# A token mixer whose normalised input is made once, split anew, and read by nearly all of its products

## The chip, the cores and the metric

The kernel runs on one core of one Trainium2 chip. The time is the device time of one execution in microseconds (us); of several runs the median counts. The five engines of the core are TensorE (PE in the profile), VectorE (DVE), ScalarE (ACT), GpSimd (POOL) and SyncE (SP), which issues most of the DMAs. Each engine works through its own instructions in the order in which they are written and waits at the first one whose inputs or buffers are not ready.

## The reference, cut to what matters

A decoder trunk of two layers over 512 tokens and 1024 features, in fp32. In each layer the mixer normalises its input, multiplies it by one wide matrix, and cuts the columns of the result into the inputs of three branches and three gates:

```python
def rmsnorm(x, w):
    r = lax.rsqrt(jnp.mean(xf * xf, axis=-1, keepdims=True) + EPS)
    return (xf * r * w.astype(jnp.float32)).astype(x.dtype)

def hybrid_mix(u, w_in, ...):
    (u_s5, q, k, v, g_out, gate_lr, z, xbc, dt_raw,
     gate_s5, gate_gla, gate_ssd) = jnp.split(u @ w_in, split_pts, axis=-1)
    y_s5 = s5_mixer(u_s5, ...)
    y_gla = gla_mixer(q, k, v, g_out, gate_lr, ...)
    y_ssd = ssd_mixer(z, xbc, dt_raw, ...)
    merged = (jax.nn.sigmoid(gate_s5) * (y_s5 @ w_br_s5)
              + jax.nn.sigmoid(gate_gla) * (y_gla @ w_br_gla)
              + jax.nn.sigmoid(gate_ssd) * (y_ssd @ w_br_ssd))
    return merged @ w_out

for i in range(DEPTH):
    h = h + 0.5 * swiglu(rmsnorm(h, ffn1_norm[i]), ...)
    h = h + hybrid_mix(rmsnorm(h, mix_norm[i]), w_in[i], ...)
    h = h + 0.5 * swiglu(rmsnorm(h, ffn2_norm[i]), ...)
    h = h + sigmoid(rmsnorm(h, ple_norm[i]) @ ple_gate[i]) * (p[i] @ ple_proj[i])
```

S5 is a diagonal state-space model with a gated output, GLA a gated linear attention in chunks, SSD the Mamba-2 mixer with a short convolution.

## The kernel before

Features lie on the 128 partitions and the 512 tokens along the row, so one tile of a feature block is 128x512. The residual h is eight such tiles. Each fp32 product is made of three matmuls of a faster type: both operands are split into a high and a low part, and `mm3` (L214, L219, L220) adds high by high, high by low and low by high. A pair of output tiles with 1024 inputs is 48 such matmuls of 512 columns.

Weights stream from memory over SyncE's queue into `raw` (three buffers); ScalarE makes the high part `wh` (L187) and VectorE the low part `wl` (L188). Products go into five PSUM banks `ps`; smaller work shares three banks `pa`. Tiles in SBUF come from a fixed set of slots (`self.T`, `self.free`), so a tile can also wait for the last reader of the slot that it gets.

The norm's root r is not applied to the input of the mixer's products. `prenorm` splits the input times the norm's weight at once, without r, into X (high parts `xh`, low parts `xl`), so that the products can begin before r is known. r, spread over all partitions, is multiplied in where a result leaves PSUM: by VectorE in `plain` (L1104, with a factor L1106), in `uev` (L1122, which also transposes) and in `gate` (L1230); the gate's Tanh is then ScalarE's (L1231).

`spread` brings a row of roots to all partitions: ScalarE and VectorE make `hl`, VectorE a diagonal `dg` (L288), TensorE multiplies it by ones (L290), and ScalarE copies the result (L292). Ahead of it `colsum` sums squares by TensorE (L271) and VectorE transposes the sums (L273). GLA's output o goes through both, is multiplied by the spread root `rb` (L1181), and split into `yh` and `yl` for its branch product.

S5 goes through eight blocks. In a block TensorE makes the states' inputs (L722), ScalarE and VectorE turn and scan them (`xsw`, `W`, `Hh`), and TensorE reads them a block later (L703) into Y, which ScalarE copies (L708). After blocks 3 and 7 eight DMAs write Y to memory (L711). Four loads (L756) bring it back as `y5`; gelu is two ScalarE and two VectorE steps a tile (L764 to L767), the result is split into `ggh` and `ggl`, and these feed the gated product (`s5_glu`). In SSD, `w` is made by ScalarE (L1055, L1056) and VectorE (L1057) and read by L1067.

The mixer's order of emission is a table written by hand, `ORDER`. A name in it is a unit (`lrdt`, `v0`, `kq0`, `bc0`, `x0`, `z0`, `glu` and so on), or one further step of a generator: `g0`, `g1` for GLA's halves, `st` for the SSD states, `s5_`, `s0`, `s1` for the SSD groups, `A`, `B`, `C` for the branches of GLA, S5 and SSD. A scheduler then places the instructions of all engines; it may move ready products between others. The units marked `first` are placed ahead of others that are ready.

Of the kernel before, what the change touches and what calls it, by code (L numbers as in the profile page):

```python
# [94 lines left out]
class Trunk:  # L95
# [988 lines left out]
    def mix(self, l, prep):  # L1084
# [135 lines left out]

        def branch(bi, Y):

            c0, wn = ((D, "w_br_gla"), (0, "w_br_s5"), (2 * D, "w_br_ssd"))[bi]
# [187 lines left out]
```

## Time and profile before

| | us |
|---|---|
| median of three runs | 2515.77 (2513.34 to 2517.47) |
| profiled execution | 2515.53 |
| its span | 2513.4 |
| TensorE busy | 2480.5 |
| VectorE busy | 1685.9 |
| ScalarE busy | 1041.3 |
| GpSimd busy | 50.1 |

Busy times are those of one execution and overlap; an engine at 99% of the span leaves 33 us in which it stood still. Matmuls are pipelined, so a matmul's own duration in a row is longer than the step from one to the next.

### The profile page before, as it was taken

The page shows a single profiled execution, that of the slowest core. Times are in us where ns is not written, and L with a number is a line of the kernel's source. Part 1 is how long each engine was busy: PE and PEld are TensorE (multiplying, and loading weights), DVE is VectorE, ACT ScalarE, POOL GpSimd, SP SyncE. Part 2 cuts the span into 40 slices and gives each one's busy share as a digit, 9 for nine tenths or more (in the row PEclk, how much of TensorE's full clock was granted, in tenths as well). Part 3 has the DMA queues.
Part 4 walks back from the last instruction along what each step waited for, and adds up shares of the span by engine and source line. Part 5 has one row for each costly group of instructions (what it writes and reads, how often), then busy time and mean ns, then how long its engine had stood idle before and what let it go on. Part 6 is the DMA issues. An engine that isn't in the chain of part 4 may idle for free.

```text
span 2513.4 us, 34868 instructions
## 1 busy us (share of the span) xinstructions
PE 2480.5 (99%) x12724; PEld 2044.5 (81%) x12724; DVE 1685.9 (67%) x4087; ACT 1041.3 (41%) x1889; POOL 50.1 (2%) x101
## 2 busy tenths in 40 slices
PE   9999999989999999999999999999899999999998
PEld 7888888868888888888888888888688888888888
DVE  7866778987776544445787577789876755434556
ACT  5323345545544433234533233455465434322354
POOL 0000000010000000000000000000100000000000
PEclk9999999989999999999999999999999999999999
DMA  4444345344223333333334444553442222323242
GB/s 166 126 132 125 114 132 150 115 140 144 90 84 101 100 93 101 93 92 97 109 101 121 131 129 118 155 126 110 145 142 91 86 101 93 101 93 101 79 127 76
DMA packets 164525, 284.54 MB, mean 113 GB/s; under 512 B 88321, under 2 KB 94337, under 8 KB 164353
## 3 DMA queue, kind: packets, MB, share of 16 engines
q1 hardware_dynamic: 157824, 261.31, 34.6%
q0 software_dynamic: 6528, 21.01, 2.6%
q8 instruction: 99, 1.62, 0.3%
q14 instruction: 74, 0.60, 0.1%
HBM read 258.64 MB, written 23.63 MB: 112 GB/s over the span
## 4 chain that ended last, share of the span: by engine, by line
PE 96%; DVE 2%; DMA 0%; issue 0%; ACT 0%; SPq 0%; DVEq 0%; ACTq 0%
PE ps L214 30%; PE ps L219 30%; PE ps L220 30%; PE ps L1168 1%; PE ps L1167 1%; PE ps L1166 1%; PE pa L849 1%; PE pa L703 1%; PE pa L1067 0%; PE pa L271 0%; DMA raw<-in_w 0%; PE pa L909 0%; DVE attn L855 0%; PE pa L722 0%; PE ps L217 0%
## 5 line engine op out<-in xcount | busy, mean ns | idle before, releaser
L188 DVE TENSOR_TENSOR wl<-raw,wh 128x512 fp32r<-128x512 f32 (+1 forms) x856 | 579.3, 678 | 574.0 <-ACT wh L187 567.9
L187 ACT ACTIVATE wh<-raw 128x512 fp32r<-128x512 f32 (+1 forms) x856 | 531.1, 622 | 996.3 <-PE ps L220 919.3
L214 PE MATMUL ps<-xh,wh 128*128 128x512 f32 (+1 forms) x2336 | 898.7, 385 | 0.9 <-ACT wh L187 0.9
L219 PE MATMUL ps<-xh,wl 128*128 128x512 f32 (+1 forms) x2336 | 898.2, 385 | 0.0
L220 PE MATMUL ps<-xl,wh 128*128 128x512 f32 (+1 forms) x2336 | 896.8, 384 | 0.0
L214 PEld LDWEIGHTS ps<-xh,wh 128*128 128x128 f32 x2336 | 439.0, 188 | 89.6 <-issue 1.5
L219 PEld LDWEIGHTS ps<-xh,wl 128*128 128x128 f32 x2336 | 439.1, 188 | 87.5 <-issue 1.5
L220 PEld LDWEIGHTS ps<-xl,wh 128*128 128x128 f32 x2336 | 438.9, 188 | 87.1 <-DVE xl L303 0.5
L214 PE MATMUL ps<-hdh,wh 128*128 128x512 f32 x704 | 274.3, 390 | 0.0
L220 PE MATMUL ps<-hdl,wh 128*128 128x512 f32 x672 | 261.5, 389 | 0.0
L219 PE MATMUL ps<-hdh,wl 128*128 128x512 f32 x672 | 261.4, 389 | 0.0
L214 PEld LDWEIGHTS ps<-hdh,wh 128*128 128x128 f32 x704 | 132.1, 188 | 28.4 <-issue 1.2
L220 PEld LDWEIGHTS ps<-hdl,wh 128*128 128x128 f32 x672 | 126.1, 188 | 26.3
L219 PEld LDWEIGHTS ps<-hdh,wl 128*128 128x128 f32 x672 | 126.1, 188 | 26.1
L343 ACT ACTIVATE s<-g 128x512 f32<-128x512 f32 x88 | 55.5, 631 | 100.3 <-DVE g L342 100.2
L227 ACT ACTIVATE hdh<-hd 128x512 fp32r<-128x512 f32 x88 | 55.5, 630 | 91.7 <-DVE hd L345 91.7
L344 DVE TENSOR_TENSOR u<-ps,r 128x512 f32<-128x512 f32 x88 | 60.6, 689 | 36.7 <-PE ps L220 36.2
L231 DVE TENSOR_TENSOR hdl<-hd,hdh 128x512 fp32r<-128x512 f32 x88 | 60.6, 688 | 31.8 <-ACT hdh L227 31.5
L214 PE MATMUL ps<-yh,wh 128*128 128x512 f32 x192 | 75.8, 396 | 0.1
L219 PE MATMUL ps<-yh,wl 128*128 128x512 f32 x192 | 75.1, 391 | 0.0
L220 PE MATMUL ps<-yl,wh 128*128 128x512 f32 x192 | 74.1, 394 | 0.0
L342 DVE TENSOR_TENSOR g<-ps,r 128x512 f32<-128x512 f32 x88 | 60.5, 688 | 7.8 <-ACT r L292 6.1
(381 smaller groups left out, 2544.9 us busy)
## 6 DMA issues: line engine op xcount, KB each, us to landing
raw<-in_w SPq DMA_DIRECT2D x414, 512.0 KB, 3.5
mat<-st SPq DMA_DIRECT2D x64, 64.0 KB, 2.3
mat<-toep SPq DMA_DIRECT2D x16, 256.0 KB, 2.2
mat<-cs SPq DMA_DIRECT2D x16, 256.0 KB, 3.4
raw<-in_w SPq DMA_DIRECT2D x16, 256.0 KB, 2.6
St<-mat POOLq DMA_DIRECT2D x16, 256.0 KB, 4.1
CS<-mat POOLq DMA_DIRECT2D x16, 256.0 KB, 4.6
Tt<-mat POOLq DMA_DIRECT2D x16, 256.0 KB, 4.8
```

The source lines that it names most:

```text
L187: nc.scalar.activation(H, x, AF.Copy)
L188: nc.vector.tensor_tensor(L, x, H.bitcast(F32), ALU.subtract)
L214: mm(ps, H[:, j, c], XH[k], start=(k == 0), stop=False)
L219: mm(ps, L[:, j, c], XH[k], start=False, stop=False)
L220: mm(ps, H[:, j, c], XL[k], start=False, stop=(k == nk - 1))
L227: nc.scalar.activation(H, x, AF.Copy)
L231: nc.vector.tensor_tensor(L, x, H.bitcast(F32), ALU.subtract)
L342: nc.vector.tensor_tensor(g1, pg, r[:p], ALU.mult)
L343: nc.scalar.activation(s, g1, AF.Silu)
L344: nc.vector.tensor_tensor(u1, pu, r[128 - p:], ALU.mult)
L703: nc.tensor.matmul(py[j:j + 64, g * 64:g * 64 + 64], x[:, g * 128 + j:g * 128 + j + 64], y, start=x is Tt, stop=x is Ot)
L849: nc.tensor.matmul(ps[o:o + 64, c * 64:c * 64 + 64], d[:, c * 128 + o:c * 128 + o + 64], P.rearrange("p (f c b j) -> p c b f j", f=2, c=4, ...
```

## The change

A new unit `xn` makes the normalised input itself once r is there: for each of the eight feature blocks GpSimd multiplies h by r (`xt`), ScalarE rounds `xt` times the norm's weight to the high part, and VectorE takes the low part. All products through `feats` after it read this XN in place of X. `lrdt`, both `v` and `kq0` keep X, which a second new unit, `xo`, frees after `v1`. Results of products on XN need no r: `plain` and `uev` are then one ScalarE activation each, and a gate is one Tanh straight from PSUM. The gates are no longer made inside the branches but by three generators `gA`, `gB`, `gC`, and are kept until their branch takes them. The table is written anew.

```diff
--- before.py
+++ after.py
@@ -37,10 +37,12 @@
 HALVES = ((0, 12), (12, NF))
 
 
 ORDER = """
-    lrdt v0 kq0 g0 g0 st s5_ g0 g0 kq1 g0 s5_ g0 st g0 g1 off go0 g0 v1 g0 g0 g1 st g0 bc0 gla0 g1 g1 go1 g1 g1 g1
...
+    lrdt v0 kq0 xn g0 g0 st v1 xo s5_ g0 g0 kq1 g0 s5_ g0 st g0 g1 off go0 g0 g0 g0 g1 st g0 gA gla0 g1 g1 go1 g1 g1 gA
...
+    s0 s0 s5_ gB s0 s0 s5_ s0 s0 s5_ z1 glu cb1 s1 gB s1 s1 gB s1 s1 B s1 s1 B gC s1 s1 B gC s1 s1 B s1 gC gC C C C C
 """
 
 
@@ -1093,14 +1095,32 @@
         def feats(evac, *cols):
             W = self.wunit(*[("w_in", c) for c in cols])
             ps = [self.PS(), self.PS()]
-            self.mm3([(ps[j], c128(j)) for j in range(2)], W, X)
+            self.mm3([(ps[j], c128(j)) for j in range(2)], W, XN or X)
             with self.first():
                 for j in range(2):
                     evac(j, ps[j])
 
+        XN = []
+
+        def normal():
+
+            H, L = [], []
+            for k in range(KD):
+                t = self.T("xt")
+                nc.gpsimd.tensor_tensor(t, self.hs[k], r, ALU.mult)
+                H.append(self.T("xh", F32R))
+                L.append(self.T("xl", F32R))
+                w = vec[:, VEC["mix"]][:, k:k + 1]
+                nc.scalar.activation(H[k], t, AF.Copy, scale=w)
+                v.scalar_tensor_tensor(L[k], t, w, H[k].bitcast(F32), ALU.mult, ALU.subtract)
+                self.free(t)
+            XN.extend((H, L))
+
         def plain(name, ps, scale=None):
             t = self.T(name)
-            if scale is None:
+            if XN:
+                nc.scalar.activation(t, ps, AF.Copy, scale=scale or 1.0)
+            elif scale is None:
                 v.tensor_tensor(t, ps, r, ALU.mult)
             else:
                 v.scalar_tensor_tensor(t, ps, scale, r, ALU.mult, ALU.mult)
@@ -1119,7 +1139,7 @@
             def uev(ps):
                 t = self.T("u")
                 sw = "p (c s) -> p c s"
-                v.tensor_tensor(t.rearrange("p (s c) -> p c s", s=8), ps.rearrange(sw, s=8), r.rearrange(sw, s=8), ALU.mult)
+                nc.scalar.activation(t.rearrange("p (s c) -> p c s", s=8), ps.rearrange(sw, s=8), AF.Copy)
                 u.append(t)
             for m in (0, 2):
                 feats(lambda j, ps: uev(ps), _span(C_U + m * 128))
@@ -1218,19 +1238,27 @@
         ygl, ysd, steps = [], [], []
         M, MH, ML = [None] * KD, [], []
 
+        ready = [deque() for _ in range(3)]
+
+        def gates(bi):
+
+            for d in range(0, KD, 2):
+                gt = []
+
+                def gate(j, ps):
+                    g = self.T("gate")
+                    nc.scalar.activation(g, ps, AF.Tanh, scale=0.5)
+                    gt.append(g)
+                feats(gate, _span(C_G + (D, 0, 2 * D)[bi] + d * 128))
+                ready[bi].append(gt)
+                yield
+
         def branch(bi, Y):
 
-            c0, wn = ((D, "w_br_gla"), (0, "w_br_s5"), (2 * D, "w_br_ssd"))[bi]
+            wn = ("w_br_gla", "w_br_s5", "w_br_ssd")[bi]
             Y = self.splits(Y(), "y")
             for d in range(0, KD, 2):
-                gt = []
-
-                def gate(j, ps):
-                    g = self.T("gate")
-                    v.tensor_tensor(g, ps, r, ALU.mult)
-                    nc.scalar.activation(g, g, AF.Tanh, scale=0.5)
-                    gt.append(g)
-                feats(gate, _span(C_G + c0 + d * 128))
+                gt = ready[bi].popleft()
                 W = self.wunit((wn, _span(d * 128)), n=512)
                 ps = [self.PS(), self.PS()]
                 self.mm3([(ps[j], c128(j)) for j in range(2)], W, Y)
@@ -1273,17 +1301,17 @@
 
         gr, vt, gt, got = [[], []], [[], []], [[], []], {}
         gens = {"g0": gla(0), "g1": gla(1), "st": self.ssd_steps(l, lambda: got["lrdt"][0], steps), "s5_": s5(), "s0": ssd(0), "s1": ssd(1),
-                "A": branch(0, lambda: ygl), "B": branch(1, lambda: got["glu"]), "C": branch(2, lambda: ysd)}
+                "A": branch(0, lambda: ygl), "B": branch(1, lambda: got["glu"]), "C": branch(2, lambda: ysd), "gA": gates(0), "gB": gates(1), "gC": gates(2)}
         units = {"lrdt": lrdt_in, "kq": kq_in, "v": lambda t: v_in(t, vt[t]), "go": lambda t: go_in(t, gt[t]),
                  "gla": lambda t: gla_out(*gr[t]), "bc": bc_in, "x": x_in, "z": z_in, "cb": lambda g: self.ssd_load(g, steps[4]),
-                 "off": lambda: self.free(*got["lrdt"]), "glu": lambda: self.s5_glu(l, got["y5"], got["gx"])}
+                 "off": lambda: self.free(*got["lrdt"]), "xn": normal, "xo": lambda: self.free(*X[0], *X[1]), "glu": lambda: self.s5_glu(l, got["y5"], got["gx"])}
         for name in ORDER.split():
             if name in gens:
                 next(gens[name], None)
                 continue
             u = name.rstrip("01")
             got[name] = units[u](*(int(x) for x in name[len(u):]))
-        self.free(*X[0], *X[1])
+        self.free(*XN[0], *XN[1])
         for d in range(0, KD, 2):
             W = self.wunit(("w_out", _span(d * 128)))
             ps = [self.PS(), self.PS()]
```

In the new kernel the lines up to the mixer stand two further down (L703 is now L705, L722 is L724, L290 is L292, L708 is L710); L1122 is `plain`, L1250 the gate's Tanh.

On TensorE, at the end of GLA's second half in layer 0, the old kernel has this order (`attn,v` and `qe,gst` are the last products of GLA, `sq,ones` is `colsum`, `dg,ones` the spread, `U,St` and `U,Tt` are S5's):

```order
L896 MATMUL pa<-v,kT 64x128 x6
L722 MATMUL pa<-U,St 64x64 x8
L703 MATMUL pa<-U,Tt 64x64 x2
...
L909 MATMUL pa<-attn,v 128x128 x8
L914 MATMUL pa<-qe,gst 128x128 x6
L271 MATMUL pa<-sq,ones 32x128 x8
L290 MATMUL pa<-dg,ones 128x512 x2
L722 MATMUL pa<-U,St 64x64 x8
L703 MATMUL pa<-U,Tt 64x64 x2
```

The new one has at the same place, from the last products of GLA on, and then from `colsum` to the first product that reads the split o (`yh`; the `yh` rows before it are of the other half):

```order
L221 MATMUL ps<-xh,wl 128x512
L911 MATMUL pa<-attn,v 128x128 x8
L916 MATMUL pa<-qe,gst 128x128 x2
L222 MATMUL ps<-xl,wh 128x512
L216 MATMUL ps<-xh,wh 128x512
...
L273 MATMUL pa<-sq,ones 32x128 x8
L216 MATMUL ps<-yh,wh 128x512
...
L222 MATMUL ps<-xl,wh 128x512
L292 MATMUL pa<-dg,ones 128x512 x2
L216 MATMUL ps<-yh,wh 128x512
```

Products with 512 columns now stand between GLA's last steps, 24 of them between `colsum` and the spread; behind the spread the first `yh` of the second half follows at once.

On TensorE at the end of S5 in layer 0, the old kernel has products of a branch (`yh`) and of SSD's inputs (`xh`) between the last L703 and the gated products (`ggh`):

```order
L703 MATMUL pa<-Hh,Ot 64x64 x2
L1025 MATMUL pa<-cst,conv 128x128 x2
L220 MATMUL ps<-xl,wh 128x512
L214 MATMUL ps<-xh,wh 128x512
...
L1015 MATMUL pa<-conv 128x128 x4
L214 MATMUL ps<-ggh,wh 128x512
```

The new one:

```order
L705 MATMUL pa<-Hh,Ot 64x64 x2
L1069 MATMUL pa<-w,xd 64x128 x7
L1074 MATMUL pa<-conv,xd 128x128 x3
L1069 MATMUL pa<-w,xd 64x128 x7
L216 MATMUL ps<-ggh,wh 128x512
L221 MATMUL ps<-ggh,wl 128x512
```

The 512-column rows between the two are gone from there; fourteen small matmuls on `w` and three on `conv` are what is left.

On ScalarE at the same place, the old kernel copies the last Y (from `pa_6668`) behind three `w` steps:

```order
L1231 ACTIVATE gate_6844<-gate_6844 128x512
L1052 ACTIVATE E_6740<-cb_5816 64x512
L1052 ACTIVATE E_6740<-cb_5817 64x512
L1055 ACTIVATE w_6742<-cb_5816,cum_4395 128x128 x3
L708 ACTIVATE Y_6310<-pa_6668 128x256
```

The new kernel copies it (from `pa_7026`) behind these:

```order
L710 ACTIVATE Y_6698<-pa_6983 128x256
L994 ACTIVATE th_6941<-conv_6940 128x512
L1057 ACTIVATE w_7136<-cb_6618,cum_4443 128x128 x4
L1057 ACTIVATE w_7002<-cb_6616,cum_4443 128x128 x4
L1058 ACTIVATE w_7136<-w_7136 128x512
L1058 ACTIVATE w_7002<-w_7002 128x512
L766 ACTIVATE y52_7211<-y5_7152 128x512
L710 ACTIVATE Y_6698<-pa_7026 128x256
L766 ACTIVATE y52_7216<-y5_7153 128x512
L768 ACTIVATE y52_7211<-y52_7211 128x512
```

Two whole `w` tiles and the first gelu square now stand ahead of the last copy of Y; the squares of the first two `y5` tiles, which need only Y's first half, stand around it.

## Rows read from the trace of the kernel before

**Rows 1.** The page's first part: busy time, share, instructions of each engine.

```profile
PE 2480.5 (99%) x12724; PEld 2044.5 (81%) x12724; DVE 1685.9 (67%) x4087; ACT 1041.3 (41%) x1889; POOL 50.1 (2%) x101
```

**Rows 2.** Windows: stretch, length, busy PE, PEld, DVE, ACT, POOL, granted clock, DMA share, GB/s.

```profile
515.00:530.00 15.00, 12.47 (x134) 10.63 (x133) 13.82 (x39) 6.28 (x14) 2.66 (x5) 0.89 0.51 158
530.00:545.00 15.00, 7.80 (x105) 5.88 (x105) 10.42 (x35) 6.02 (x14) 3.72 (x7) 0.65 0.38 124
1759.00:1774.00 15.00, 12.54 (x148) 10.49 (x148) 13.84 (x39) 6.28 (x14) 2.66 (x5) 1.00 0.50 155
1774.00:1789.00 15.00, 7.47 (x100) 5.65 (x97) 11.59 (x38) 6.59 (x17) 3.71 (x7) 0.77 0.39 128
600.00:640.00 40.00, 40.00 (x274) 32.16 (x273) 30.97 (x58) 29.05 (x63) 2.14 (x4) 1.00 0.50 138
```

**Rows 3.** TensorE's waits: what waited for what, us in total, times, longest.

```profile
PE pa L290 <- DVE dg L288: 10.3, 2, 5.2
...
PE ps L214 <- ACT wh L187: 0.9, 1, 0.9
```

**Rows 4.** The chain of waits, 515 to 546: start, us, engine, line.

```profile
533.87 0.70 PE pa L271 x8
...
538.85 0.70 DVE dg L288
...
539.69 1.36 PE pa L290 x2
...
543.81 0.51 PE pa L722 x16
...
544.86 0.23 PE ps L219
```

**Rows 5.** Groups of layer 0's mixer (365 to 795): busy, mean ns, idle before.

```profile
L188 DVE TENSOR_TENSOR wl<-raw,wh 128x512 fp32r<-128x512 f32 x134 | 91.5, 686 | 49.2 <-ACT wh L187 48.7
...
L1230 DVE TENSOR_TENSOR gate<-ps,r 128x512 f32<-128x512 f32 x23 | 15.6, 687 | 6.1 <-PE ps L220 4.6 <-PE pa L290 1.5
...
L735 DVE TENSOR_TENSOR_SCAN W<-m,xsw 128x64 f32<-128x64 f32 x32 | 6.7, 270 | 0.1
...
L991 DVE SCALAR_TENSOR_TENSOR conv<-xbc,chalf,conv 128x510 f32<-128x510 f32 x8 | 5.9, 740 | 0.0
...
L1122 DVE TENSOR_TENSOR u<-ps,r 128x512 f32<-128x512 f32 x4 | 4.3, 1080 | 0.3 <-PE ps L220 0.3
...
L740 DVE TENSOR_TENSOR W<-CS,W 128x256 f32<-128x256 f32 x8 | 3.4, 426 | 4.1 <-ACT W L738 4.0
```

**Rows 6.** Timeline, 392 to 397: start, us, engine, line.

```profile
393.75 0.60 ACT L292 ACTIVATE r<-pa 128x512 f32<-128x512 f32 x1
```

**Rows 7.** GpSimd's groups of the whole run.

```profile
L1141 POOL MEMSET lrs<- 128x512 f32 x2 | 1.1, 530 | 132.9 <-PE ps L219 132.9
```

**Rows 8.** Timeline, 540 to 546: the spread root of GLA and the split.

```profile
540.49 1.20 ACT L292 ACTIVATE rb<-pa 128x512 f32<-128x512 f32 x2 [1.86 <-PE pa L290]
...
541.12 1.29 DVE L1181 TENSOR_TENSOR o<-o,rb 128x512 f32<-128x512 f32 x2 [0.98 <-ACT rb L292]
...
541.84 0.63 ACT L227 ACTIVATE yh<-o 128x512 fp32r<-128x512 f32 x1 [0.16 <-DVE o L1181]
```

**Rows 9.** Timeline, 616 to 641: ScalarE and SyncE's queue at S5's end.

```profile
617.91 0.36 ACT L708 ACTIVATE Y<-pa 128x256 f32<-128x256 f32 x1
618.17 1.56 ACT L1055 ACTIVATE w<-cb,cum 128x128 f32<-128x128 f32 x5
618.30 3.87 SPq L711 DMA_DIRECT2D ys<-Y  x8
...
620.16 0.62 ACT L1056 ACTIVATE w<-w 128x512 f32<-128x512 f32 x1
...
622.28 2.40 SPq L756 DMA_DIRECT2D y<-ys  x3
```

**Rows 10.** The loads of y5, line L756.

```profile
DMA to landing us min/median/max: 2.6/3.0/5.8
```

More of the change, by code (lines that the diff above doesn't have):

```diff
@@ L40 @@
 ORDER = """
-    lrdt v0 kq0 g0 g0 st s5_ g0 g0 kq1 g0 s5_ g0 st g0 g1 off go0 g0 v1 g0 g0 g1 st g0 bc0 gla0 g1 g1 go1 g1 g1 g1
-    s5_ g1 g1 g1 x0 s5_ g1 z0 cb0 gla1 s5_ s5_ s0 A s5_ s0 bc1 s5_ s0 A s5_ A s5_ s0 s5_ s0 s0 cb1 s0 s0 s0 s0 s0
-    A s5_ s5_ x1 s1 s1 s1 s1 glu z1 B s0 s1 s1 B s1 s1 s1 B s1 s1 s1 C C C B C
+    lrdt v0 kq0 xn g0 g0 st v1 xo s5_ g0 g0 kq1 g0 s5_ g0 st g0 g1 off go0 g0 g0 g0 g1 st g0 gA gla0 g1 g1 go1 g1 g1 gA
+    g1 g1 gA g1 g1 bc0 g1 gA gla1 A s5_ A x0 s5_ A z0 s5_ A s5_ bc1 s5_ cb0 s0 s0 s5_ gB s0 s0 s5_ s0 s0 x1 s5_
+    s0 s0 s5_ gB s0 s0 s5_ s0 s0 s5_ z1 glu cb1 s1 gB s1 s1 gB s1 s1 B s1 s1 B gC s1 s1 B gC s1 s1 B s1 gC gC C C C C
 """
@@ L1219, in mix @@
         M, MH, ML = [None] * KD, [], []
-        def branch(bi, Y):
-            c0, wn = ((D, "w_br_gla"), (0, "w_br_s5"), (2 * D, "w_br_ssd"))[bi]
-            Y = self.splits(Y(), "y")
+        ready = [deque() for _ in range(3)]
+        def gates(bi):
             for d in range(0, KD, 2):
@@ L1229, in gate, with branch @@
                     g = self.T("gate")
-                    v.tensor_tensor(g, ps, r, ALU.mult)
-                    nc.scalar.activation(g, g, AF.Tanh, scale=0.5)
+                    nc.scalar.activation(g, ps, AF.Tanh, scale=0.5)
                     gt.append(g)
-                feats(gate, _span(C_G + c0 + d * 128))
+                feats(gate, _span(C_G + (D, 0, 2 * D)[bi] + d * 128))
+                ready[bi].append(gt)
+                yield
+        def branch(bi, Y):
+            wn = ("w_br_gla", "w_br_s5", "w_br_ssd")[bi]
+            Y = self.splits(Y(), "y")
+            for d in range(0, KD, 2):
+                gt = ready[bi].popleft()
                 W = self.wunit((wn, _span(d * 128)), n=512)
```

## The prediction

> **What bounds the kernel now.** I read the page's first part first: TensorE is busy for 2480.5 of 2513.4 us, VectorE for 67% and ScalarE for 41% [rows 1]. So work taken from VectorE is worth nothing in itself; only places count where TensorE stands still. The windows show where: in layer 0 TensorE is busy 12.47 of the 15 us from 515 and 7.80 of the 15 us from 530, at a granted clock of 0.89 and 0.65; in layer 1 it is 12.54 and 7.47, at 1.00 and 0.77. Elsewhere in the mixer it is dense (40.00 of 40 from 600) [rows 2]. Idle in the four windows: 2.53 + 7.20 + 2.46 + 7.53 = 19.7 us. Busy time at a low clock is slower work too: 12.47 x 0.11 + 7.80 x 0.35 + 7.47 x 0.23 = 5.8 us. Together **25.5 us**, the most the change can take out.
>
> The chain of waits says what stands there. At the end of GLA's second half TensorE sums the squares of o (`colsum`, L271), and VectorE then goes alone through `sums`, some fifteen tiny square-root steps and `dg`, while TensorE waits for the spread L290 [rows 4]; the wait for `dg` is the largest of its list, 10.3 us in two pieces [rows 3]. TensorE works in order, and no product stands there that could fill the time. Before it VectorE is behind with `attn`, `z` and `wl`.
>
> **The change part by part.**
>
> *Evictions.* Both layers together lose 92 VectorE evictions: 84 at 0.69 us (step 0.60, since two overlap: L1181, two in 1.29) [rows 5, 8] and the 8 transposing `u` at 1.08 [rows 5]; they gain 16 `xl` steps, priced like L991's 0.74 (step 0.66) [rows 5]. That is -84 x 0.60 - 8 x 1.0 + 16 x 0.66 = -48 us of VectorE. ScalarE gains 16 `xh` and 44 evictions; an activation out of PSUM is 0.60 (L292, two in 1.20) [rows 8], so +36 us; the 48 gates stay one Tanh each. ScalarE's transposing `u` is in no row: between 0.60 and VectorE's 1.08. I take 0.60, since ScalarE has slack there; at 1.08 it is 4 us over both layers, hidden under the products of u. TensorE's instructions are the same in number, so all this is hidden by TensorE, except where its order waits.
>
> *Eight GpSimd products `xt` in each layer.* No row has one. Nearest are GpSimd's own 128x512 memset at 0.53 [rows 7] and VectorE's two-input 0.69 [rows 5]. `r` is there at 394.35 [rows 6]; by the new order the first product that reads XN starts 51 matmuls of 0.227 us = 11.6 us later, and its last k about 7.6 us after that. From 19 us I leave 1.3 for `xh` and `xl`: eight steps may take 2.2 us each before TensorE waits. At 0.53 or 0.69 they cost nothing, and I take that. [...]
>
> *The end of GLA.* Gate, xbc and branch products now stand between L911 and the spread L292 (lines of the new kernel), some 50 matmuls: the 5.0 us from the end of `colsum` to `dg` [rows 4] are covered by 24 of them, 24 x 0.227 = 5.4 us [rows 4]. Both layers: **-25.5**. What comes behind is new: right after the spread the order asks for `yh` of the same o. From the spread this takes `rb` 0.60, o x rb 0.69, `yh` 0.63 [rows 8], with the hops 2.2 us, and nothing fills them: **+4.4** in both layers. Bounds: 1 us each if the spread comes early, 4 if `dg` is late.
>
> *The end of S5.* This is the dear part. In the old order x1 and four s1 steps stand between the last L703 and the gated products of S5 (`ggh`); in the new one only the tail of ssd(0). I lay TensorE's new rows end to end (0.227 a product [rows 4]; the small ones near 0.06, as 8 of L722 in 0.51 [rows 4], where a row of the order is two in the profile). From block 7's L724 to the first L705 that reads its `Hh`: 5.5 us. In that time VectorE's order has 3 xsw (0.34 each), 3 conv STT (0.66), 4 scans (0.19), 3 `wl` (0.60), one w (0.60), one E (0.47), W twice, Hh, a last conv STT (0.60) [rows 5]: 8.4 us, after about 1.2 us of TensorE and ScalarE. So `Hh` is 9.6 - 5.5 = **4.1 us late**, and TensorE stands.
>
> W, which stands ahead of `Hh`, is there 8.7 us after block 7's L724. It releases what ScalarE has ahead of the last Y copy: eight L1057 (0.29 each: five in 1.56), two L1058 and one gelu square (0.53 each), then the copy itself, 0.36 [rows 9]: 4.3 us, so the copy ends at 13.0. Laid end to end it would end at 6.7, 0.3 us after the last L705: 6.3 late. Then eight DMA issues, 3.9 us [rows 9], their landing, and the load of y5, 2.6 to 5.8 with 3.0 in the middle [rows 10]. In the old order the copy at 617.91 leads to the loads' issue at 622.28 [rows 9]; two of the four loads are now issued ahead of the writes. Copy to third load: 0.4 + 3.9 + 2.1 + 2.6 = 9.0 us. Its gelu and split, three steps on ScalarE and two on VectorE, 3.0. By the dense count, `ggh` of the third tile is asked for 9.9 us after the last L705, but it needs 0.3 + 6.3 + 9.0 + 3.0 = 18.6: **8.7 us late** in all (the 4.1 and 6.3 are in it). I take 9.0 a layer, **+18**; the free products there are one gate pair, since S5's four sums hold four of the five `ps` buffers. Bounds: 4 if VectorE catches up (then 0.3 + 2 + 9 + 3 against 9.9), 16 if the fourth load takes 5.8, all queues come late, and the clock falls.
>
> *Clock.* The old stall brought the clock down [rows 2]; a 9 us stall cut in pieces may do so too. I add 1 us a layer: **+2**.
>
> Sum: -25.5 + 4.4 + 18 + 2 = **-1 us**. The profiled execution is 2515.53 against a median of 2515.77 (2513.34 to 2517.47), so I forecast **2514.5**. No change is told from one here by less than 0.2%, 5 us.
>
> **The rivals.**
>
> 1. *The new stall is short (faster).* If VectorE, 24 us a layer lighter, comes early to S5's last block, `Hh` is not late and the writes start at once: 4 instead of 9 a layer and no low clock. -25.5 + 4.4 + 8 = -13: **2502.5**. For it: VectorE's total; against it: my count of rows just there, 9.6 us for 5.5. It decides when `Hh` comes less than 1 us late.
>
> 2. *ScalarE becomes the late engine (slower).* Between Y copies of blocks 5 and 7, the new order gives ScalarE 35 rows: 12 L1057, 4 `wh`, 3 L1058, 3 evictions or gates, 2 L1054, 6 half-width S5 copies and some more, by an estimate from the steps above 15.5 us, for 11.6 us of TensorE. If it comes there late already, those 3.9 us stand on top of 9, the fourth load adds up to 2.8, and the clock falls: 16 a layer. -25.5 + 4.4 + 32 = +11: **2526.5**. It decides when the copy of Y is over 10 us late. [...]
>
> 3. *GpSimd is slow.* Above 2.2 us a step the products of u wait: at 3.5, 8 x 1.3 = 10 us a layer, +20 on the forecast: **2535**. Both nearest rows are far below.
>
> 4. *The change does not do what it says.* The fill at GLA's end is not ready in time, because its weights wait for ScalarE behind the new evictions, and the old stall stays beside the new: 2515.5 + 4.4 + 18 = **2538**. Against it: weights are hardly in the list of waits, 0.9 us for `wh` in the whole run [rows 3].
>
> **How the numbers follow.** The forecast has 0.40 (its own range 2510 to 2521, so nearly all of it is no change), the short stall 0.32, the late ScalarE 0.23, slow GpSimd 0.03, the old stall kept 0.02. Faster by over 0.2%: 0.33; within: 0.37; slower: 0.30. The range takes both bounds of S5's end, 4 us less one for a neat spread and 16 with a late `dg`: 2500 to 2530.
>
> **What would show it.** The waits for `dg` and the half clock at GLA's end must be gone. TensorE should wait for `yh` about 2 us a layer, and for `Hh`, w and `ggh` at the end of S5 about 9 in all, with the third `ggh` the last to come. `xt` under 2.2 us each. The forecast is wrong if TensorE stays dense through S5's end, or if a product waits for `wh` there for long.

## The result and the profile after

The changed kernel takes 2532.8 us, the median of four runs (2529.01 to 2535.16), against 2515.55 for the kernel before in the same comparison: ratio 1.0068, interval 1.0056 to 1.008. That is **slower by 17 us**, outside the predicted range and of the other sign. The profiled execution took 2535.16 us, with a span of 2533.4. Its first part of the page, as [rows 1]:

```profile
PE 2493.7 (98%) x12724; PEld 2050.9 (81%) x12724; DVE 1655.0 (65%) x4011; ACT 1075.0 (42%) x1949; POOL 79.6 (3%) x117
```

VectorE's busy time fell by 30.9 us, where I had counted 48, and ScalarE's rose by 33.7, where I had counted 36. TensorE's waits, in the list by what was waited for (total, times, longest), as [rows 3]:

```profile
PE pa L705 <- DVE E L1077: 5.4, 2, 2.7
PE pa L273 <- DVE sq L1229: 4.0, 2, 2.1
PE ps L216 <- ACT yh L229: 3.0, 2, 1.5
PE pa L705 <- DVE Hh L746: 2.6, 2, 1.3
PE ps L222 <- DVE yl L233: 2.5, 2, 1.3
...
PE ps L222 <- DVE xl L1115: 1.2, 2, 0.6
```

The wait for `dg`, 10.3 us before, has left the top of the list; shorter ones stand there. The windows say what they cost. Columns are as in [rows 2]: TensorE's busy time stands second, its granted clock third from the end.

```profile
515.00:545.00 30.00, 30.00 (x220) 23.44 (x219) 21.56 (x47) 11.89 (x21) 3.22 (x6) 1.00 0.41 128
545.00:560.00 15.00, 12.98 (x61) 9.61 (x60) 7.60 (x22) 4.60 (x11) 1.08 (x2) 0.89 0.18 62
655.00:665.00 10.00, 6.76 (x76) 5.29 (x76) 9.64 (x25) 9.78 (x22) 0.00 (x0) 1.00 0.29 75
665.00:675.00 10.00, 7.96 (x69) 6.62 (x70) 7.48 (x16) 9.11 (x21) 0.00 (x0) 0.66 0.55 131
675.00:685.00 10.00, 7.26 (x36) 5.02 (x34) 7.62 (x14) 5.66 (x11) 0.02 (x1) 0.91 0.22 60
685.00:695.00 10.00, 9.76 (x34) 7.90 (x34) 5.24 (x21) 1.54 (x5) 1.58 (x3) 0.75 0.42 131
```

I count as the prediction did: idle time, plus busy time by what the granted clock lacks of 1.00. What a low clock does stands in the same trace: from one 512-column product to the next it is 0.43 us in 686 to 689, at a granted clock of 0.50, and 0.23 us in 691 to 694, at 1.00. The place of the old stall (first line) is dense at full clock. The new wait behind the spread (second line) costs 2.02 + 12.98 x 0.11 = 3.4 us. The end of S5 (last four lines) costs 8.26 idle and 7.96 x 0.34 + 7.26 x 0.09 + 9.76 x 0.25 = 5.8 by the clock, 14.1 us. In layer 1 the same two places cost 3.4 and 11.3. Of the 25.4 us at the end of S5 in both layers, 15.5 are idle time and 9.9 the clock.

The chain of the same stretch shows the end of S5 in order of time (start, us, what):

```profile
670.13 0.28 ACT Y L710
...
673.78 3.52 DMA ys<-Y
677.48 2.80 DMA y<-ys
...
681.55 0.52 ACT sq L1228
682.07 0.26 ACT th L1132
...
683.63 1.04 ACT wh L189 x2
684.67 0.53 ACT ggh L229
```

The last Y copy leads to eight writes, the writes to the third load, the load to gelu, and a square, a Tanh and two weight halves stand on ScalarE ahead of the third `ggh`. For that `ggh` itself TensorE waits only 0.24 us. Its longest wait in this last part is for `sq`, SSD's squares. ScalarE's order has the second of them behind the first gelu step, and there ScalarE stood still for the load (ScalarE's and TensorE's timelines):

```profile
680.30 1.25 ACT L766 ACTIVATE y<-y 128x512 f32<-128x512 f32 x2 [3.33 <-DMA y<-ys]
681.46 0.61 ACT L1228 ACTIVATE sq<-ysd 128x512 f32<-128x512 f32 x1
683.03 0.56 PE L273 MATMUL pa<-sq,ones 128*32 128x128 f32 x8 [2.12 <-DVE sq L1229]
```

The second square's input was there at 678.58. So the late load costs TensorE time through what stands behind gelu on ScalarE.

VectorE was to be relieved. Grouped by line, in the 16 us after r, it shows this (count, busy us, mean ns):

```profile
L1115 DVE SCALAR_TENSOR_TENSOR xl<-xt,vec,xh 128x512 fp32r<-128x512 f32 x5 | 7.5, 1516 | 0.2 <-ACT xh L1114 0.2
L190 DVE TENSOR_TENSOR wl<-raw,wh 128x512 fp32r<-128x512 f32 x4 | 5.0, 1242 | 0.7 <-ACT wh L189 0.7
L1169 DVE TENSOR_TENSOR lrs<-lrdt,lrs 16x512 fp32r<-16x512 f32 x1 | 1.7, 1691 | 0.0
L1124 DVE TENSOR_TENSOR kq<-ps,r 128x512 f32<-128x512 f32 x1 | 0.7, 683 | 0.0
```

And GpSimd's timeline beside it (start, us):

```profile
394.33 14.68 POOL L1110 TENSOR_TENSOR xt<-h,r 128x512 f32<-128x512 f32 x8 [34.18 <-ACT r L294]
408.94 0.66 POOL L800 DMA_DIRECT2D w<-in_gla_w  x1
```

While GpSimd makes its eight products, VectorE's steps with two inputs in SBUF (`xl`, `wl`, `lrs`) take 1.2 to 1.7 us in the mean, where [rows 5] had 0.69 for `wl`; the step that reads PSUM (`kq`) took 0.68, as it did in the kernel before. The prediction did not see this. At the start it went the other way. VectorE's timeline has, after a step on `lrdt` of 0.68 us:

```profile
396.18 0.68 DVE L826 TENSOR_TENSOR qk<-kq 128x512 f32<-128x512 f32 x1
396.79 0.73 DVE L1115 SCALAR_TENSOR_TENSOR xl<-xt,vec,xh 128x512 fp32r<-128x512 f32 x1
```

These three, with two inputs in SBUF as well, kept their time, and GpSimd's second product, which ran beside them, took 3.10 us where the first took 1.31.

### The profile page after: what moved, and what is told of

It reads as the page before. It is cut to its first block, busy times and chain, and to the rows that moved or that the text cites. A ratio compares the mean times of both kernels' runs of the same rounds, so it can differ in the third digit from the quotient of the medians.

```text
span 2533.4 us, 34857 instructions
## 1 busy us (share of the span) xinstructions
PE 2493.7 (98%) x12724; PEld 2050.9 (81%) x12724; DVE 1655.0 (65%) x4011; ACT 1075.0 (42%) x1949; POOL 79.6 (3%) x117
## 4 chain that ended last, share of the span: by engine, by line
PE 88%; issue 4%; DVE 4%; ACT 3%; DMA 1%; SPq 0%; POOL 0%; DVEq 0%; POOLq 0%; ACTq 0%
PE ps L216 29%; PE ps L222 28%; PE ps L221 28%; DVE wl L190 1%; DMA y<-ys 0%; PE pa L851 0%; PE pa L705 0%; DVE d L867 0%; ACT wh L189 0%; PE pa L724 0%; DVE d L874 0%; DVE attn L857 0%; DVE xl L1115 0%; PE pa L911 0%; DVE d L866 0%
```

## The experiments

Two theories stood at the start. By the first the new table is dear: the end of S5 is worse than counted. By the second XN is: GpSimd's products hold up VectorE, or delay what stands behind them on GpSimd's queue. The times, with the kernel before in the same comparison at 2514.72 to 2515.55 us:

| kernel | table | XN | `xt` on | us | ratio (interval) |
|---|---|---|---|---|---|
| changed | new | yes | GpSimd | 2532.8 | 1.0068 (1.0056 to 1.008) |
| e1 | old | yes | GpSimd | 2531.2 | 1.0068 (1.0051 to 1.0085) |
| e2 | new | no | | 2518.57 | 1.0015 (1.0006 to 1.0024) |
| e3 | new, S5 filled | yes | GpSimd | 2525.46 | 1.0044 (1.0029 to 1.0059) |
| e5 | new, `x0` early | yes | GpSimd | 2520.37 | 1.0022 (1.0012 to 1.0031) |
| e4 | new | yes | VectorE | 2524.26 | 1.0035 (1.0024 to 1.0047) |
| e7 | old | no | 8 unread | 2548.01 | 1.0131 (1.0116 to 1.0147) |
| e6 | both of e3, e5 | yes | GpSimd | 2512.85 | 0.9995 (0.9986 to 1.0005) |
| e8 | both | no | | 2514.98 | 0.9999 (0.999 to 1.0009) |
| e9 | both | yes | VectorE | 2508.41 | 0.9971 (0.9961 to 0.9982) |
| e10 | old | no | 26 memsets | 2548.64 | 1.0133 (1.0118 to 1.0148) |
| e11 | old | yes | VectorE | 2526.68 | 1.0047 (1.003 to 1.0064) |
| e12 | new, GLA load first | yes | GpSimd | 2534.29 | 1.0076 (1.0061 to 1.0091) |
| e13 | old | no | 8 unread, later | 2529.66 | 1.006 (1.0043 to 1.0077) |
| e14 | both, GLA load first | yes | GpSimd | 2521.49 | 1.0024 (1.0015 to 1.0033) |

### Table or arithmetic: e1 and e2

e1 keeps the new arithmetic and goes back to the old table, with `xn` behind `kq0`, `v1` and `xo` early, and each gate step right ahead of its branch step:

```diff
-    lrdt v0 kq0 xn g0 g0 st v1 xo s5_ g0 g0 kq1 g0 s5_ g0 st g0 g1 off go0 g0 g0 g0 g1 st g0 gA gla0 g1 g1 go1 g1 g1 gA
...
+    lrdt v0 kq0 xn g0 g0 st v1 xo s5_ g0 g0 kq1 g0 s5_ g0 st g0 g1 off go0 g0 g0 g0 g1 st g0 bc0 gla0 g1 g1 go1 g1 g1 g1
+    s5_ g1 g1 g1 x0 s5_ g1 z0 cb0 gla1 s5_ s5_ s0 gA A s5_ s0 bc1 s5_ s0 gA A s5_ gA A s5_ s0 s5_ s0 s0 cb1 s0 s0 s0 s0 s0
+    gA A s5_ s5_ x1 s1 s1 s1 s1 glu z1 gB B s0 s1 s1 gB B s1 s1 s1 gB B s1 s1 s1 gC C gC C gC C gB B gC C
```

> The arithmetic of the change alone: XN and the evictions by ScalarE, in the old order (xn stands behind kq0, v1 and xo early, the gates right ahead of their branch step). Theory (the order is at fault: it asks for S5's gated products right behind S5's last block): the old stall at GLA's end stays, about 25 us over both layers, no stall at S5's end, time 2510 to 2518. Rival (ScalarE, loaded with the evictions and the split of XN, is late wherever products end): slower than before by 8 us or more, 2524 to 2535, with TensorE waiting for wh or for Y.

e2 keeps the new table and takes XN away: X is kept, and VectorE multiplies by r as before.

```diff
+            return
...
-                nc.scalar.activation(t.rearrange("p (s c) -> p c s", s=8), ps.rearrange(sw, s=8), AF.Copy)
+                v.tensor_tensor(t.rearrange("p (s c) -> p c s", s=8), ps.rearrange(sw, s=8), r.rearrange(sw, s=8), ALU.mult)
...
-                    nc.scalar.activation(g, ps, AF.Tanh, scale=0.5)
+                    v.tensor_tensor(g, ps, r, ALU.mult)
+                    nc.scalar.activation(g, g, AF.Tanh, scale=0.5)
...
```

> The new order alone: no XN, every product reads X, results and gates leave PSUM through VectorE times r as before. Theory (order): the stall at S5's end stays and is a little longer, since VectorE has 24 us more a layer, 2532 to 2545. Rival (ScalarE's evictions make Y, and so the loads of y5, late): the last copy of Y comes earlier and the time falls back to 2510 to 2522.

The table alone costs +3.7 us (2518.57 against 2514.89); XN in the old table costs +16.3, in the new one 14.2 more. So the theory of the dear table fell as the main cause. Its time is that of its rival, but the stall at S5's end stays, as its theory had it. Windows of e2 at the spread, S5's end and the branch of S5:

```profile
541.00:561.00 20.00, 19.31 (x98) 15.41 (x97) 13.31 (x34) 8.33 (x17) 1.07 (x2) 1.00 0.30 85
650.00:700.00 50.00, 44.40 (x275) 35.85 (x272) 45.51 (x95) 33.55 (x68) 2.14 (x4) 0.86 0.41 117
720.00:740.00 20.00, 18.38 (x94) 14.87 (x95) 17.49 (x30) 14.81 (x34) 0.00 (x0) 1.00 0.26 79
```

The wait at S5's end is there without XN as well: 5.60 + 44.40 x 0.14 = 11.8 us. With VectorE doing the evictions, it is late all the same.

### The end of S5 and the branch order: e3 and e5

e3 moves `x1` and two gate steps behind the last S5 step, so that 72 products of 512 columns stand between the last L705 and `ggh`:

```diff
-    g1 g1 gA g1 g1 bc0 g1 gA gla1 A s5_ A x0 s5_ A z0 s5_ A s5_ bc1 s5_ cb0 s0 s0 s5_ gB s0 s0 s5_ s0 s0 x1 s5_
-    s0 s0 s5_ gB s0 s0 s5_ s0 s0 s5_ z1 glu cb1 s1 gB s1 s1 gB s1 s1 B s1 s1 B gC s1 s1 B gC s1 s1 B s1 gC gC C C C C
+    g1 g1 gA g1 g1 bc0 g1 gA gla1 A s5_ A x0 s5_ A z0 s5_ A s5_ bc1 s5_ cb0 s0 s0 s5_ s0 s0 s5_ s0 s0 s5_ s0
+    s0 s5_ s0 s5_ s5_ s0 x1 gB s0 s0 s0 z1 gB glu cb1 s1 gB s1 s1 gB s1 s1 B s1 s1 B gC s1 s1 B gC s1 s1 B s1 gC gC C C C C
```

> The changed kernel with another order at S5's end: S5's last blocks are asked for earlier, and the products of x1, z1 and one pair of gates stand between the last L705 and the gated products, 72 matmuls of 512 columns where there were none (16 us). Theory (order): the 27 us lost at S5's end in both layers shrink to under 6, time 2506 to 2514. Rival (VectorE and ScalarE are simply behind there, whatever stands on TensorE): the lateness goes over to the evictions of x1 and z1 and to SSD, under 8 us is won, 2525 to 2533.

e5 puts the products of `x0` between GLA's end and its first branch step, where TensorE waits for `yh`:

```diff
-    g1 g1 gA g1 g1 bc0 g1 gA gla1 A s5_ A x0 s5_ A z0 s5_ A s5_ bc1 s5_ cb0 s0 s0 s5_ gB s0 s0 s5_ s0 s0 x1 s5_
+    g1 g1 gA g1 g1 bc0 g1 gA gla1 x0 A s5_ A s5_ A z0 s5_ A s5_ bc1 s5_ cb0 s0 s0 s5_ gB s0 s0 s5_ s0 s0 x1 s5_
```

> The changed kernel with the product x0 moved ahead of GLA's branch, so that it stands between GLA's end and the first product that reads the split o. Theory: the wait for yh and yl behind the spread and the low clock that follows, 7.4 us over both layers, go: 2524 to 2528. Rival: the conv of x0, now earlier on VectorE and ScalarE, makes GLA's end or S5's blocks later by as much: 2530 to 2536.

e3 wins 7.3 us of the changed kernel, so little as its rival had it: TensorE then waits at S5's end for evictions of the fill (`xbc` 2.9 us in both layers, a gate 1.3) and still for `Hh` (2.5). e5 wins 12.4, more than either expectation. Its place held 6.9 (the window 545 to 560 is now dense at full clock); of the rest, 1.5 is the wait for `sq`, which fell from 4.0 to 2.5, and where the other 4.0 lie is not shown. e6 has both edits:

```diff
+    g1 g1 gA g1 g1 bc0 g1 gA gla1 x0 A s5_ A s5_ A z0 s5_ A s5_ bc1 s5_ cb0 s0 s0 s5_ s0 s0 s5_ s0 s0 s5_ s0
+    s0 s5_ s0 s5_ s5_ s0 x1 gB s0 s0 s0 z1 gB glu cb1 s1 gB s1 s1 gB s1 s1 B s1 s1 B gC s1 s1 B gC s1 s1 B s1 gC gC C C C C
```

> The changed kernel with both earlier edits of the order, x0 ahead of GLA's branch and the fill between S5's last block and its gated products. Theory (two places, each paid by itself): the gains add, 12.4 + 7.3 us below the changed kernel, 2510 to 2516. Rival (the second edit only wins what the first has already won by lighter queues): 2517 to 2521.

It comes to 2512.85, 20.0 us below the changed kernel, about the sum of the two (19.7), and level with the kernel before. So fill wins the loss back, but that is no proof of who made the waits late.

### GpSimd beside VectorE: e4, e7, e10 and e13

e4 is the changed kernel with `xt` on VectorE:

```diff
-                nc.gpsimd.tensor_tensor(t, self.hs[k], r, ALU.mult)
+                v.tensor_tensor(t, self.hs[k], r, ALU.mult)
```

> The changed kernel with the eight products xt made by VectorE in place of GpSimd. In the changed kernel VectorE's two-input steps took 1.5 to 1.8 us in place of 0.7 while GpSimd worked on xt, some 7 us lost a layer. Theory (GpSimd's products slow VectorE, and a late VectorE is what the XN costs): those steps are back at 0.7, VectorE does 8 x 0.6 = 4.8 us more but loses none of the 7, 2525 to 2532. Rival (XN costs because its steps stand in VectorE's order early, in the stage in which it is late anyway): 4.8 us more a layer, 2538 to 2546.

VectorE gets 16 steps more and the kernel is 8.5 us faster (2524.26). VectorE's busy time is 1650.9 us, 4.1 less than in the changed kernel in spite of the 16 steps. VectorE by line, in the same window as above:

```profile
L1115 DVE SCALAR_TENSOR_TENSOR xl<-xt,vec,xh 128x512 fp32r<-128x512 f32 x8 | 5.7, 752 | 0.0
L1110 DVE TENSOR_TENSOR xt<-h,r 128x512 f32<-128x512 f32 x8 | 4.9, 677 | 0.0
```

All eight `xt` and eight `xl` take 10.6 us; with GpSimd five `xl` alone took 7.5. From r to the first `yh` behind the spread in layer 0 (the changed kernel, then e4) TensorE does the same work:

```profile
394.24:552.32 158.08, 154.14 (x968) 124.28 (x966) 128.73 (x335) 90.57 (x174) 21.63 (x22) 1.00 0.40 111
393.44:548.13 154.69, 152.73 (x967) 124.11 (x965) 126.54 (x342) 89.93 (x172) 6.10 (x12) 1.00 0.41 113
```

The changed kernel needs 3.4 us more, 2.0 of them idle. But e4 takes away two things at once: the products beside VectorE, and what they hold up on GpSimd's queue, since GLA's first weight load goes out at 359.82 in place of 408.94. The windows of e4 at the three places of e2:

```profile
541.00:561.00 20.00, 18.40 (x85) 14.27 (x85) 12.57 (x33) 7.72 (x16) 1.08 (x2) 0.91 0.24 75
650.00:700.00 50.00, 42.61 (x264) 33.90 (x263) 40.02 (x87) 34.94 (x72) 2.13 (x4) 0.86 0.36 96
720.00:740.00 20.00, 18.37 (x89) 14.39 (x87) 12.68 (x21) 12.49 (x30) 0.00 (x0) 0.91 0.22 65
```

Against e2, XN without GpSimd costs here (1.60 + 1.7) - 0.69 = 2.6 us, 13.4 - 11.8 = 1.6, and 1.65 by the clock alone.

e7 is the kernel before with eight GpSimd products added behind r that nothing reads:

```diff
-    lrdt v0 kq0 g0 g0 st s5_ g0 g0 kq1 g0 s5_ g0 st g0 g1 off go0 g0 v1 g0 g0 g1 st g0 bc0 gla0 g1 g1 go1 g1 g1 g1
+    lrdt v0 kq0 xn g0 g0 st s5_ g0 g0 kq1 g0 s5_ g0 st g0 g1 off go0 g0 v1 g0 g0 g1 st g0 bc0 gla0 g1 g1 go1 g1 g1 g1
...
+        def idle_mults():
+            t = self.tp.tile([128, N], F32, name="xt", tag=f"z{self.idle[-1]}", bufs=1)
+            for k in range(KD):
+                nc.gpsimd.tensor_tensor(t, self.hs[k], r, ALU.mult)
```

> The old kernel with eight products of h by r on GpSimd right after r is made, in each layer; nobody reads their result. Theory (GpSimd's work slows VectorE): VectorE's two-input steps in those 15 us take 1.5 to 1.8 us, it comes 7 us later to GLA's end in each layer, 2522 to 2532. Rival (the loss comes from xh and xl waiting in order for xt, not from the GpSimd work itself): no change, 2512 to 2518.

It loses 33 us and mixes two causes: VectorE's steps are slow again (`lrs` 1.69), and GLA's first weight load, a DMA that GpSimd issues, comes at 407.73 in place of 360.34. e10 takes the second cause alone: 26 memsets in place of the products, started by one column of a product.

```diff
+            nc.gpsimd.tensor_tensor(t[:, :1], self.hs[0][:, :1], r[:, :1], ALU.mult)
+            for k in range(26):
+                nc.gpsimd.memset(t, 0.0)
```

> The old kernel with 26 GpSimd memsets of 128x512 in each layer in the place of the eight products of the earlier run, started by r as well, about the same 14 us of GpSimd, which read nothing. Theory (the loss is VectorE's two-input steps beside GpSimd's two-input products): VectorE's steps stay at 0.7 us and most of the 33 us goes, 2513 to 2522. Rival (the loss is GpSimd's own queue: the load of GLA's second weight and a memset stand behind it, and GLA starts late): 2538 to 2550.

GpSimd's timeline and VectorE's `wl` by line:

```profile
394.37 15.11 POOL L1222 MEMSET xt<- 128x512 f32 x26
409.64 0.64 POOL L798 DMA_DIRECT2D w<-in_gla_w  x1 [0.17 <-issue]
```
```profile
L188 DVE TENSOR_TENSOR wl<-raw,wh 128x512 fp32r<-128x512 f32 x6 | 4.1, 688 | 6.9 <-ACT wh L187 6.9
L1149 DVE TENSOR_TENSOR lrs<-lrdt,lrs 16x512 fp32r<-16x512 f32 x1 | 0.7, 683 | 0.0
```

Beside the memsets VectorE's steps keep their time (`wl` 0.69, `lrs` 0.68), yet the kernel loses the same 33 us: in the old table what stands behind on GpSimd's queue suffices for all of e7's loss. GpSimd's rows stand in order: it stood still for 34.54 us until r came, the memsets ran from 394.37 to 409.48, and GLA's first load followed at 409.64, where the kernel before has it at 360.34. So that load is 49 us late and not 15; GLA's second load and S5's first four are some 28 us late (S5's first goes out at 410.45 in place of 381.96). In e7 and e10 rows of the other engines stand in another order too; their share is not told apart. e13 therefore takes the first cause alone: the eight unread products stand behind both GLA loads, and the orders of TensorE, VectorE, ScalarE and SyncE are those of the kernel before, row for row.

```diff
-    lrdt v0 kq0 g0 g0 st s5_ g0 g0 kq1 g0 s5_ g0 st g0 g1 off go0 g0 v1 g0 g0 g1 st g0 bc0 gla0 g1 g1 go1 g1 g1 g1
+    lrdt v0 kq0 g0 g0 st s5_ g0 g0 kq1 g0 s5_ g0 st g0 g1 xn off go0 g0 v1 g0 g0 g1 st g0 bc0 gla0 g1 g1 go1 g1 g1 g1
```

> The old kernel with the eight unread GpSimd products of the earlier run, placed behind the loads of both GLA halves and of S5's first block on GpSimd's queue; the order of every other engine is that of the old kernel, row for row. Theory (queue): VectorE's steps in those 14 us still take 1.5 to 1.8 us, but of the 33 us at most 4 are left, 2514 to 2519. Rival (slowed steps, 7 us a layer in a stage in which VectorE is late): 2524 to 2532.

It loses 14.5 us. The products waited for their buffer and ran from 456.96 to 468.27. VectorE's timeline there (start, us), with GpSimd's rows ahead:

```profile
456.96 11.31 POOL L1221 TENSOR_TENSOR xt<-h,r 128x512 f32<-128x512 f32 x8 [71.54 <-DVE xb L812]
473.45 0.58 POOL L684 DMA_DIRECT2D St<-mat  x1 [5.18 <-PE pa L975]
```
```profile
458.45 5.61 DVE L816 TENSOR_TENSOR_SCAN b<-ones,xb 128x128 f32<-128x128 f32 x4
463.99 1.73 DVE L188 TENSOR_TENSOR wl<-raw,wh 128x512 fp32r<-128x512 f32 x1
```

and the same rows of the kernel before:

```profile
457.85 1.37 DVE L816 TENSOR_TENSOR_SCAN b<-ones,xb 128x128 f32<-128x128 f32 x4
459.14 0.67 DVE L188 TENSOR_TENSOR wl<-raw,wh 128x512 fp32r<-128x512 f32 x1
```

Each step is longer by 1.06 us (a scan 1.40 in place of 0.34), close to one GpSimd product (1.30 at the median here); at its next L870 VectorE was 8.1 us later than before (473.03 against 464.95), of which it had 0.6 when the stretch began. GpSimd itself stood idle for 5.18 us before its next load, so its queue held nothing back. So eight products that nothing reads, and that move no other engine's order, cost 14.5 / 2 = 7.2 us a layer. That is the theory of the slowed VectorE, shown by itself, in the old table.

The three kernels beside one another: `wl` took 1.73 us beside products in e13 and 0.69 beside memsets in e10, and `kq`, out of PSUM, took 0.68 beside products in the changed kernel. In the changed kernel it is one side or the other: VectorE's steps became longer by up to 1.1 us (`wl` 1.80 in place of 0.69), or GpSimd's product went from 1.31 to 3.10. What decides which, no run here shows.

### GLA's load in the changed kernel: e12 and e14

e12 lets GLA's first step, with its load, go ahead of `xn`; e14 does the same in e6.

```diff
-    lrdt v0 kq0 xn g0 g0 st v1 xo s5_ g0 g0 kq1 g0 s5_ g0 st g0 g1 off go0 g0 g0 g0 g1 st g0 gA gla0 g1 g1 go1 g1 g1 gA
+    lrdt v0 kq0 g0 xn g0 st v1 xo s5_ g0 g0 kq1 g0 s5_ g0 st g0 g1 off go0 g0 g0 g0 g1 st g0 gA gla0 g1 g1 go1 g1 g1 gA
```

> The changed kernel with GLA's first step asked for ahead of xn, so that the load of GLA's second weight and its memset stand ahead of the eight xt on GpSimd's queue; GpSimd still makes xt. Theory (the cost of GpSimd's work is its queue: GLA starts some 10 us later in each layer): most of the 8.5 us that xt by VectorE won comes here too, 2520 to 2526. Rival (VectorE's slowed steps are the cost): 2529 to 2534.

> The order of the run with both edits, with GLA's first step ahead of xn and xt on GpSimd. Theory (queue): as good as or better than xt by VectorE (2508.4), since VectorE is spared 4.8 us a layer, 2503 to 2509. Rival (slowed steps): no better than the run with both edits, 2511 to 2514.

Neither gains: 2534.29, level with the changed kernel, and 8.6 us worse than e6. The load went out at 360.50, but VectorE's `lrs` still took 1.68. VectorE's first scan of GLA came earlier than in the changed kernel, yet later than in e4 (changed, e12, e4):

```profile
426.15 1.37 DVE L818 TENSOR_TENSOR_SCAN b<-ones,xb 128x128 f32<-128x128 f32 x4
420.44 1.37 DVE L818 TENSOR_TENSOR_SCAN b<-ones,xb 128x128 f32<-128x128 f32 x4
411.77 1.37 DVE L818 TENSOR_TENSOR_SCAN b<-ones,xb 128x128 f32<-128x128 f32 x4
```

But the edit also moves rows of the other engines, and a new wait stands in the list of e12. Below it is the stretch in which it lies, of the changed kernel and of e12:

```profile
PE ps L216 <- ACT v L1191: 4.6, 2, 2.3
```
```profile
405.00:435.00 30.00, 29.38 (x136) 23.39 (x136) 25.75 (x72) 25.89 (x48) 7.74 (x11) 1.00 0.41 140
405.00:435.00 30.00, 26.55 (x112) 20.78 (x110) 27.88 (x81) 25.40 (x46) 6.68 (x9) 0.89 0.38 117
```

Here e12 loses 3.45 + 26.55 x 0.11 = 6.4 us, the changed kernel 0.6, and 1.3 in the 45 us behind it, where e12 loses nothing. So a gain from the earlier load can be hidden under the new stall, and e12 does not tell the queue from the slowed steps: what share of the 8.5 us is the queue's stays open. In e14 the same stretch loses 3.46 + 26.54 x 0.06 = 5.1 us, 3.2 more than the two stretches of e6; in both layers that is 6.3 of its 8.6.

### XN without GpSimd in three tables: e8, e9 and e11

e8 is e6 without XN (the edits of e2), e9 is e6 with the edit of e4, e11 is e1 with it.

> The same order as the run with both edits, but without XN: all products read X and leave PSUM through VectorE times r, as in the old kernel. Theory (the order is worth something, XN costs more than it gives): faster than the old kernel, 2502 to 2510. Rival (in this order VectorE, with its evictions, is late at S5's end): 2514 to 2520, no better than with XN.

> The order of the run with both edits, and xt made by VectorE in place of GpSimd. Theory (the order's two places and GpSimd's work are three separate costs): some 8 us below the run with both edits (2512.9), 2502 to 2508, faster than the old kernel. Rival (what VectorE wins early it had won already by the fill): 2510 to 2514, no change.

> The arithmetic of the change in the old order, as in the first run, with xt made by VectorE in place of GpSimd. Theory (GpSimd's work is the larger part of the 16 us that the arithmetic cost in the old order): 2514 to 2522. Rival (the split of XN and the evictions by ScalarE cost it, whoever makes xt): 2528 to 2534.

e8 falls to its rival: fill does nothing for the old evictions that the old table did not do. e11 lies between its two expectations. In the table of e6, XN with `xt` on VectorE and evictions by ScalarE is 6.6 us faster than none (2508.41 against 2514.98); with `xt` on GpSimd it is 2.1, which the intervals do not part from nothing. In the old table it costs 11.2 even so. **e9 beats both kernels**, by 7.1 and by 24 us. Its waits are short and spread out, the longest 2.2 us in the whole run.

## Why the prediction was wrong

**Two steps failed.** The first is the price of XN: "At 0.53 or 0.69 they cost nothing, and I take that." The prediction asked only whether TensorE would wait for XN's tiles, which it put at 2.2 us a product. That bound held: a product took 1.87 us in the mean, and TensorE waited 1.2 us in all for `xl`. What was not asked is who runs beside GpSimd and what stands behind it on its queue. The two together are shown by e4 (8.5 us by the medians, in the new table), e6 against e9 (4.4) and e1 against e11 (4.5); the slowed steps alone by e13 (14.5, in the old kernel). The eight `xl` a layer were counted among VectorE's hidden steps as well, by their sum over the run; in the old table XN without GpSimd still costs 11.2. That their early place, in GLA's stage, does this is argued; it was not tried apart.

The second is the clock: "I add 1 us a layer: +2." It measured 14.4. Counted as the prediction counts, by places in both layers:

| place | forecast | idle | by the clock |
|---|---|---|---|
| GLA's stage (394 to 540, 1650 to 1796) | none | 4.3 | 0 |
| wait for `yh` | 4.4 | 4.0 | 2.9 |
| end of S5 | 18, clock 2 | 15.5 | 9.9 |
| branch of S5 | none | 3.3 | 1.65 |

The rows of the first and the last place in layer 0:

```profile
394.00:540.00 146.00, 144.07 (x915) 117.11 (x914) 121.11 (x309) 86.58 (x164) 21.10 (x22) 1.00 0.41 109
720.00:740.00 20.00, 18.37 (x75) 14.52 (x75) 11.62 (x22) 9.21 (x20) 0.00 (x0) 0.91 0.11 38
```

With the old stall's -25.5 that is -25.5 + 27.1 + 14.4 = +16.0, against some 17 measured. So the forecast waits were sized well, even a little too dear (19.5 for 22.4). What was missing is 7.6 us of idle time in two places that the sum does not have, and 12.4 us of clock. Behind the waits at S5's end the granted clock was 0.50 from 667 to 672 us, and 0.66 in the mean of 665 to 675.

By kernels, each against the kernel before of its own comparison, the 17.3 us come apart so: the table +3.7 (e2), XN with `xt` on VectorE 5.9 more (e4), GpSimd 7.7 more (changed). Layer 0 in the traces has the same order: the first `hd` of the feed-forward behind the mixer comes at 867.4 us before, 869.6 in e2, 874.1 in e4 and 879.0 after the change. Of the 4.9 us between the last two, 0.8 are there at r already, ahead of GpSimd's first product; 3.4 lie between r and the first `yh` behind the spread, and 0.7 behind it. Of the 3.4, 2.0 are idle time of TensorE; the other 1.4 show in no wait.

**The old stall, -25.5: right.** The window is dense at full clock, and the wait for `dg` fell to 0.8 us. The rival in which it stays had no part in it; where the fill is not in the table, in e1, that wait stands at 10.2 as before.

**The wait for `yh`, +4.4: in the right place, too small.** It is 2.0 us of idle time a layer, near the 2.2 forecast; the clock, which the sum did not have here, adds 1.4, so 6.9 in all. In e2 it was 0.69 in layer 0, at full clock.

**The end of S5, +18 and +2 for the clock: the wait right in size, the clock too small.** It measured 14.1 and 11.3, 25.4 us: 8.3 and 7.2 idle where 9.0 a layer were forecast, 5.8 and 4.1 by the clock where 1 was. That the idle time fits is in part luck. The chain was the forecast one, but three of its terms were short; TensorE found other products while it ran, and `ggh` was not what it waited for longest. Block 7's L724 stand at 654.91 to 655.4, so the dense count has the last Y copy end at about 662.3; it ended at 670.40, some 8 us late, not 6.3; from the copy to the third load took 9.9, not 9.0 (the last write 3.5, for which the sum had 2.1 without a row; the load 2.8); gelu and split took 4.9, not 3.0, since a square, a Tanh and two weight halves stood among them. TensorE's first wait there was not `Hh` but E, another VectorE tile, 2.7 us, and `Hh` only 1.3.

**Not in the sum at all**: GLA's stage, and the wait for `yl` at the branch of S5 (1.3 us a layer, and in layer 0 a clock of 0.91 in 720 to 740 us, 1.65 more). In layer 1 the same wait left the clock at 1.00 (1975 to 1995 us, 18.37 busy of 20 as in layer 0).

**The rivals.** The short stall (2502.5) fell: VectorE was late at S5's last block even without evictions. The late ScalarE (2526.5) was to decide at a Y copy over 10 us late; it was some 8. ScalarE's evictions cost little there: with all of XN the place costs 14.1 in layer 0, with VectorE's evictions 11.8 (e2), and e9 is faster than e8 with them. Slow GpSimd gave nearly the measured time (2535), but by another way: it needed over 2.2 us a product and 10 us a layer of TensorE waiting for XN; the mean was 1.87, the wait 0.6 a layer. That its number is near is luck.

**The chances.** Slower by over 0.2% had 0.30. The three rivals on that side named mechanisms in which the changed kernel's own chain is late; none had an engine slowing another.

## What to carry to other kernels

Work moved to an idle engine is not free because the idle engine has time: ask what runs beside it and slows, by the rows of the other engine in that stretch once one trace has both (e13: eight products a layer that nothing reads, 14.5 us). Before an elementwise product goes to GpSimd, look for two-input VectorE steps in the same 15 us (here seven of ten took 1.5 to 1.8 us in place of 0.69) and for DMAs queued behind it on GpSimd (here a load went out 49 us late). When a fill order and an arithmetic change come in one edit, run each alone: here the order cost 4 us and the arithmetic 14, while in the table of e6 the same arithmetic with `xt` on VectorE gained 7. When a sum has waits, give each its clock from a row with such a wait: here the clock cost 14 us beside 27 of idle time, and 2 had been allowed.

## What the runs showed of the hardware

- A VectorE step of 512 columns with two inputs in SBUF beside a GpSimd product of 128x512 took 1.5 to 1.8 us in place of 0.69 in seven cases of ten in the changed kernel (394 to 409 us) and in three of eight in e7 (394 to 408), a scan of 128x128 took 1.40 in place of 0.34 (e13); three steps in a row kept 0.68 to 0.73, and the product beside them took 3.10 in place of 1.31 (changed kernel). Beside GpSimd memsets such steps kept their time (0.69, e10), and so did steps with an input from PSUM beside products (0.68, changed kernel).
- A GpSimd product of two 128x512 fp32 tiles took 1.30 us at the least (e13) and 3.10 at the most (changed kernel, where the mean was 1.87 beside busy VectorE); the memset of 128x512 that the prediction went by took 0.53.
- DMAs that GpSimd issues went out behind its other work, in order: behind 15.11 us of memsets that waited for r, GLA's first load went out at 409.64 in place of 360.34, 49 us late, and the kernel was 33 us slower in the old table (e10).
- After waits of 1.6 us in 20 the granted clock fell in some windows and not in others: 18.38 us busy of 20 kept 1.00 in e2, 18.37 had 0.91 in e4 (720 to 740 us). In the changed kernel 18.37 busy of 20 had 0.91 in layer 0 (720 to 740) and 1.00 in layer 1 (1975 to 1995).
